# A hybrid convolution and dilated-attention layer on one core: the attention's first unit 32 convolution steps later, and GpSimd's dense-key copies behind a unit's zeros

## The chip, the cores and the metric

The kernel runs on one core of a Trainium2 chip. The metric is the device time of one execution in microseconds (us); less is better. The kernel before took 2181.21 us, the median of three runs (2176.76 to 2185.51). One more execution was profiled. The engines are named as the profile names them: PE is the matmul engine (TensorE) and PEld its weight loads, DVE is VectorE, ACT is ScalarE, POOL is GpSimd, and SP is SyncE, which here only issues DMAs.

## The reference

The input is a sequence of 4096 rows of 1024 float32 values. One combined projection of the normalised rows gives two halves of 512 columns: a gated convolution and an eight-head attention.

```python
h = rmsnorm(x, norm_w); proj = h @ w_in              # (4096, 4096)
u, g_b, g_c, z_conv, q, k, v, z_attn = split(proj, 8)
y_conv = g_b * (conv3(g_c * u) + conv_b) * silu(z_conv)     # width-3, depthwise, centred
q, k = per-head rmsnorm(q), rmsnorm(k)               # 8 heads of 64
for window, dilation in ((128, 1), (512, 4), (2048, 16)):
    # keys of one residue class mod dilation: a band of half-width 64 around each query,
    # logits / 8 + T5 relative bias, softmax -> o_i, log-sum-exp lse_i
y_attn = sum_i softmax(lse)_i * o_i * silu(z_attn)
out = x + concat(y_conv, y_attn) @ w_out
```

## The kernel before

The program has three stages. The first reads x tile by tile, normalises it, and computes q, k, v and the attention's gate, and stores them and the normalised, transposed rows (`hT_d`) in device memory. The second computes the attention and, between its pieces, the convolution half's four projections. The third joins the three dilations and multiplies by `w_out`. Products are done in float16 as a high and a low part, so that a product of two tiles is three matmuls.

The order of all instructions is written out by hand: Python calls emit instructions in program order, and every engine and every DMA queue runs its own in that order. So an instruction that waits holds back all that stand behind it on its engine. This holds for POOL and for SP too, which matters here.

**Units.** The attention is 384 units `u` of 128 queries of a pair of heads (`pr`, four pairs), in groups of eight (`b` = 0 to 7). The first 32 of each pair's 96 units have dilation 16 (`U["d"] == 16`), then come 32 each of the other two. For a unit the program does, spread over several turns of the loop over `u`:

- `q_alone(u)` (L1018): POOL copies each head's queries into `qz`, a tile whose other half is zero. It is done five turns ahead.
- `k_dense(u)` (L1031): for dilation 16 only, POOL copies strided keys into dense tiles `kd`: two copies for the first of two units, one for the second. It is done six turns ahead, while the matmuls that read them (L1044, L1045) are issued two turns ahead.
- `qk(u)` (L1044, L1045): PE makes the logits. `logits(u)` (L1057): DVE adds the bias and takes the minimum of the negated logits, into a tile `L`; for one unit in three (`by_pe(u)`: u % 3 == 1) whose keys are fewer than 256, POOL first zeroes the part of `L` that gets no keys (L1053). Both come two turns ahead.
- `exps(u)` (L1066): ACT's exponentials, one turn ahead. `tr_pe(u)` (L1086): for one unit in three, PE transposes `L`, at the end of the turn before. For the others `p_hi` and `p_lo` (L1098, L1108) make float16 parts in a tile `src`, after POOL has zeroed its dead part (L1097), and `tr(u)` (L1112) transposes it by a DMA on SP's queue.
- `av(u)` (L1123 to L1126): PE multiplies by the values, three turns later (`LAG = 3`).

**Filler.** `fill(n)` runs `n` steps of the generator `conv_gen`, each of three matmuls (L854 to L856) with 128x256 results. 32 steps make one block of 128 channels for 256 rows, and 128 steps one of 16 chunks; the whole is 2048 steps, and 24 more of the output product. A block's tail comes in the steps after it, ending in a multiply on POOL (L821). At a chunk's start `load_h` issues the load of a chunk two ahead (L398, on SP's queue). `start` steps are run before unit 0; the units below `mid` = 184 share 1024 - `start` steps, the rest share 1048, half of each unit's in either half of its turn. Units in which the next pair's queries and keys are loaded get 1.2 times as many.

**The start of the attention.** `first_loads` are 20 DMA transposes of queries and keys into `qk` (L661) on SP's queue, three at the end of the first stage and 17 after the first 17 steps of filler. `load_bias(0, 0)`, at the end of turn 4, loads two pieces of the bias on SP's queue into `wst` (L917), and POOL rearranges them into `bt0` (eight copies, L921, and four small memsets, L923).

```python
for u in range(NU):
    p_hi(u); p_lo(u); exps(u + 1); tr(u) if not by_pe(u)
    fill(pers[u] / 2)
    av(u - LAG); q_order(...); q_alone(u + 5)
    k_dense(u + 6)                    # before: here
    qk(u + 2); logits(u + 2)          # logits holds the memset of L
    fill(pers[u] / 2)
    if by_pe(u + 1): tr_pe(u + 1)
    if u == 4: load_bias(0, 0); load_bias(0, 1)
```

Of the kernel before, what the change touches and what calls it, by code (L numbers as in the profile page):

```python
# [65 lines left out]
def tile_hybrid_block(  # L66
# [593 lines left out]
    def load_stacks(pr, j, a, b):  # L660
        nc.sync.dma_start(qk_t[j][:, a:b], qk_d[a:b, pr, 128 * j:128 * j + 128], transpose=True)  # L661
# [49 lines left out]
    def c_room4():  # L711
        M["res", 1] = pb.tile([128, 1024], F32, name="bt")
        M["ja1"] = pb.tile([128, 512], F32, name="bt0")
# [12 lines left out]
    def sz_load(t):  # L726
        nc.sync.dma_start(M["sz", t % 3], sz_d[t * 128:(t + 1) * 128])
# [160 lines left out]
    def fill(n):  # L888
        state["owed"] += n
        while state["owed"] >= 1.0 and not state["done"]:  # L890
            state["owed"] -= 1.0
            if bg:
                bg.pop(0)()
            if todo:
                todo.pop(0)()
            try:
                next(dense)
            except StopIteration:
                state["done"] = True
# [97 lines left out]
    def q_order(u):  # L997

        U = units[u]
        a = 256 * U["grp"] + 32 * U["b"]  # L1000
        QN[u // 2] = [pb.tile([128, 256], F16, name=f"qn{i}", bufs=3) for i in range(2)]
        for i in range(2):
            nc.gpsimd.tensor_copy(QN[u // 2][i].rearrange("p (n r) -> p n r", r=4),
                                  qk_t[i].rearrange("p (r n) -> p n r", r=4)[:, a:a + 64])
# [8 lines left out]
    def q_alone(u):  # L1013
        U = units[u]
        q_t = QN[u // 2] if U["d"] == 1 else qk_t
        for i in range(2):
            half = slice(64 * i, 64 * i + 64)
            nc.gpsimd.tensor_copy(QZ[u % QZB][i][half], cols(q_t[i], U["qc"], half))  # L1018
# [4 lines left out]
    def k_dense(u):  # L1023
        U = units[u]
        if U["d"] != 16:
            return
        a, r = U["grp"] * (S // 4), U["b"] // 2
        if U["b"] % 2 == 0:
            KD[u // 2] = [pb.tile([128, 256], F16, name=f"kd{r}_{j}") for j in range(3)]
        for j in ((0, 1), (2,))[U["b"] % 2]:  # L1030
            nc.gpsimd.tensor_copy(KD[u // 2][j], qk_t[2 + j].rearrange("p (n r) -> p r n", r=4)[:, r, a // 4:a // 4 + 256])  # L1031

    def qk(u):
        U = units[u]
        if U["b"] == 0:
            OT[U["gi"]] = pb.tile([128, 8, 2, DH + 2], F32, name="ot", bufs=2)
        kn = U["kn"]
        both = bank(3 + u % 2, [128, 2, 256])
        p = [both[:, i] for i in range(2)]
        qc, kc = U["qc"], U["kc"]  # L1040
        q_t = QN[u // 2] if U["d"] == 1 else qk_t
        k_t = KD[u // 2] if U["d"] == 16 else qk_t[2:5]
        for i in range(2):
            nc.tensor.matmul(p[i][:, 0:kn], cols(q_t[i], qc), cols(k_t[i], kc), start=True, stop=False)  # L1044
            nc.tensor.matmul(p[i][:, 0:kn], QZ[u % QZB][i], cols(k_t[2], kc), start=False, stop=True)  # L1045
        ST[u] = p

    def logits(u):
        U = units[u]
        ot, kn, p = OT[U["gi"]], U["kn"], ST[u]  # L1050
        L = pb.tile([128, 2, 256], F32, name="L", bufs=LB)
        if by_pe(u) and kn < 256:
            nc.gpsimd.memset(L[:, :, dead(U)], 0.0)  # L1053
        L = L[:, :, U["c0"]:U["c0"] + kn]
        for i in range(2):
            bias = bt[:, U["g"] - 1, i] if U["g"] else bt0[:, i].rearrange("p a b -> p (a b)")
            nc.vector.tensor_tensor_reduce(  # L1057
                out=L[:, i], in0=p[i][:, 0:kn], in1=bias[:, U["b0"]:U["b0"] + kn],
                scale=alpha, scalar=BIG, op0=OP.add, op1=OP.min, accum_out=ot[:, U["b"], i, DH:DH + 1])
        ST[u] = L  # L1060

    def exps(u):
        U = units[u]
        ot, b, L = OT[U["gi"]], U["b"], ST[u]
        for i in range(2):
            nc.scalar.activation(L[:, i], L[:, i], AF.Exp, scale=-1.0,  # L1066
                                 bias=ot[:, b, i, DH:DH + 1], accum_out=ot[:, b, i, DH + 1:DH + 2])
# [3 lines left out]
    def by_pe(u):  # L1071
        return u % 3 == 1
# [4 lines left out]
    def dead(U):  # L1077
        c0 = 192 if U["c0"] == 0 else 0
        return slice(c0, c0 + 64)
# [8 lines left out]
    def p_hi(u):  # L1088
        U = units[u]
        if by_pe(u):  # L1090
            PT[u] = pb.tile([128, 2, 2, 2, 128], F16, name="pt", bufs=PTB)
            nc.scalar.activation(PT[u][:, 0].rearrange("p a b q -> p (a b) q"), ST[u], AF.Copy, scale=P_SCALE)
            return
        src = src_of(u)
        c = slice(U["c0"], U["c0"] + U["kn"])
        if U["kn"] < 256:
            nc.gpsimd.memset(src.rearrange("p a b c -> p (a b) c")[:, :, dead(U)], 0.0)  # L1097
        nc.scalar.activation(src[:, 0, :, c], ST[u], AF.Copy, scale=P_SCALE)  # L1098

    def p_lo(u):  # L1100
        U = units[u]
        if by_pe(u):
            hi, lo = (PT[u][:, n].rearrange("p a b q -> p (a b) q") for n in range(2))
            nc.vector.scalar_tensor_tensor(lo, ST.pop(u), P_SCALE, hi, op0=OP.mult, op1=OP.subtract)
            return
        c = slice(U["c0"], U["c0"] + U["kn"])
        src = src_of(u)
        nc.vector.scalar_tensor_tensor(src[:, 1, :, c], ST.pop(u), P_SCALE, src[:, 0, :, c], op0=OP.mult, op1=OP.subtract)  # L1108

    def tr(u):  # L1110
        PT[u] = pb.tile([128, 2, 2, 2, 128], F16, name="pt", bufs=PTB)
        nc.sync.dma_start(PT[u].rearrange("p a b c q -> p (a b c) q"), src_of(u).rearrange("p a b c -> p (a b c)"), transpose=True)  # L1112

    def av(u):
        U = units[u]
        pt = PT.pop(u)
        vt = VT[U["gi"]]
        p = bank(6 + u % 2, [128, 2, DH])
        for i in range(2):
            for j in range(2):  # L1120
                v = vt[:, U["vidx"][j], i * 128:i * 128 + 128]
                hi, lo = (pt[:, n, i, j, :] for n in range(2))
                nc.tensor.matmul(p[:, i], hi, v[:, 0:DH], start=j == 0, stop=False)  # L1123
                nc.tensor.matmul(p[:, i], hi, v[:, DH:], start=False, stop=False)  # L1124
                nc.tensor.matmul(p[:, i], lo, v[:, 0:DH], start=False, stop=j == 1)  # L1125
        nc.scalar.activation(OT[U["gi"]][:, U["b"], :, 0:DH], p, AF.Copy)  # L1126
# [14 lines left out]
            nc.scalar.dma_start(dap(o_d0[grp], base, [[R, 128], [128 * R, 8], [1, RW]]), src)  # L1141

    NU = len(units)
    start, mid = 112, 184
    weight = [1 + (0.2 if u % 96 >= 70 and u < 288 else 0) for u in range(NU)]
    pers = [w * steps / sum(ws) for ws, steps in ((weight[:mid], 1024 - start), (weight[mid:], 1024 + 24)) for w in ws]
    fill(17)
# [14 lines left out]
    for u in range(NU):  # L1162
        U = units[u]
        p_hi(u)
        p_lo(u)
        if u + 1 < NU:
            exps(u + 1)
        if not by_pe(u):
            tr(u)
        fill(pers[u] / 2)  # L1170
        if u >= LAG:
            av(u - LAG)
        if u + QZB + 2 < NU and units[u + QZB + 2]["d"] == 1 and units[u + QZB + 2]["b"] % 2 == 0:
            q_order(u + QZB + 2)
        if u + QZB + 1 < NU:
            q_alone(u + QZB + 1)
        if u + 6 < NU:
            k_dense(u + 6)
        if u + 2 < NU:
            qk(u + 2)  # L1180
        if u + 3 == NU:
            c_room2()
            sz_load(0)
        if u + 2 < NU:
            logits(u + 2)
        if u + 3 == NU:
            c_room4()
        if u > 8 and U["b"] == LAG + 1:
            o_store(U["gi"] - 1)
        if U["b"] == LAG and U["gi"] + 1 < len(groups):  # L1190
            VT[U["gi"] + 1] = load_v(*groups[U["gi"] + 1])
        fill(pers[u] / 2)
        if u + 1 < NU and by_pe(u + 1):
            tr_pe(u + 1)
        if state["done"]:
            for _ in range(4):
                if bg:
                    bg.pop(0)()
        pr = U["pr"]
        if u == 4:  # L1200
            load_bias(0, 0)
            load_bias(0, 1)
        for a, b, at, rate in CHUNKS:
            p, n = divmod(u - at, 96)
            for n in range(rate * n, min(5, rate * n + rate) if 0 <= p < 3 else 0):
                load_stacks(p + 1, n, a, b)
        n = u - LAG
        if n > 0 and n % 32 == 0 and n // 32 <= 9:
            load_bias((n - 32) // 96 + 1, order[0][(n // 32 - 1) % 3])
# [107 lines left out]
```

## Time and profile before

| what | value |
|---|---|
| median of three runs | 2181.21 us (2176.76 to 2185.51) |
| the profiled execution's own time | 2186.28 us |
| its span, first to last instruction | 2184.5 us |
| mean granted PE clock | 0.987 of full speed |
| PE busy | 2081.3 us, 95% |
| DVE, ACT, POOL busy | 66%, 49%, 39% |
| first filler step to unit 0's first matmul | 722.0 to 759.2 us |
| first and last PE transposes of a unit (L1086) | 764.5 to 1821.1 us |

In the profile "busy" of PE is the union of modelled matmul times: a matmul is drawn longer than its distance to the next one, so that a gap of PE that is shown is shorter than the time lost. In lines of waits the columns are the engine and line that waited, what ended the wait, and total us, count and longest. In a timeline they are start, duration, engine, line, operation and tiles, with idle time before it in brackets. In a table of stretches each engine's busy us stand with its number of instructions, and the granted clock, the DMA engines' share and GB/s at the end.

### The profile page before, as it was taken

The page shows a single profiled execution, that of the slowest core. Times are in us where ns is not written, and L with a number is a line of the kernel's source. Part 1 is how long each engine was busy: PE and PEld are TensorE (multiplying, and loading weights), DVE is VectorE, ACT ScalarE, POOL GpSimd, SP SyncE. Part 2 cuts the span into 40 slices and gives each one's busy share as a digit, 9 for nine tenths or more (in the row PEclk, how much of TensorE's full clock was granted, in tenths as well). Part 3 has the DMA queues.
Part 4 walks back from the last instruction along what each step waited for, and adds up shares of the span by engine and source line. Part 5 has one row for each costly group of instructions (what it writes and reads, how often), then busy time and mean ns, then how long its engine had stood idle before and what let it go on. Part 6 is the DMA issues. An engine that isn't in the chain of part 4 may idle for free. (4 is left out here: it accounts for less than half of the span.)

```text
span 2184.5 us, 48540 instructions
## 1 busy us (share of the span) xinstructions
PE 2081.3 (95%) x17462; PEld 1533.7 (70%) x17462; DVE 1441.1 (66%) x4032; ACT 1069.4 (49%) x3095; POOL 851.8 (39%) x1635
## 2 busy tenths in 40 slices
PE   7699999999999989998999999999999999999999
PEld 3244444444444778888888888888888887788887
DVE  7755666656665366766677656675667676887776
ACT  6323333433432167666677656666667674222221
POOL 0322232332323265433554346433453454343332
PEclk9899999999999999999999999999999999999999
DMA  5255489975554877799877998769977687787775
GB/s 204 88 153 174 142 176 172 221 177 161 169 169 137 179 138 164 147 164 186 164 160 137 172 194 136 153 120 176 204 141 129 122 171 225 233 256 244 244 244 183
DMA packets 692397, 378.34 MB, mean 173 GB/s; under 512 B 470721, under 2 KB 636732, under 8 KB 688060
## 3 DMA queue, kind: packets, MB, share of 16 engines
q1 hardware_dynamic: 570788, 304.72, 62.0%
q10 hardware_dynamic: 121368, 70.53, 13.7%
q8 instruction: 137, 2.24, 0.4%
q14 instruction: 104, 0.85, 0.1%
HBM read 157.77 MB, written 110.39 MB: 123 GB/s over the span
## 5 line engine op out<-in xcount | busy, mean ns | idle before, releaser
L854 PE MATMUL bank<-hb,w 128*128 128x256 f16 x2048 | 560.9, 274 | 0.3 <-ACT cu L861 0.3
L856 PE MATMUL bank<-hb,w 128*128 128x256 f16 x2048 | 560.8, 274 | 0.0
L855 PE MATMUL bank<-hb,w 128*128 128x256 f16 x2048 | 560.8, 274 | 0.0
L410 PE MATMUL bank<-wa,hb 128*128 128x512 f16 x1024 | 391.4, 382 | 14.9 <-DMA hb<-xs 11.4
L1057 DVE CUSTOM_DVE_ANT_0 L<-bank,bt,alpha 128x256 f32<-128x256 f32 (+1 forms) x768 | 319.0, 453 | 126.3 <-PE bank L1045 74.1
L1066 ACT ACTIVATE L<-L,ot 128x256 f32<-128x256 f32 (+1 forms) x768 | 364.2, 476 | 60.0 <-DVE ot L1057 58.4
L412 PE MATMUL bank<-wa,hb 128*128 128x512 f16 x1024 | 391.2, 382 | 0.8 <-DMA hb<-xs 0.7
L411 PE MATMUL bank<-wa,hb 128*128 128x512 f16 x1024 | 390.9, 382 | 0.3 <-DVE wa L301 0.2
L1018 POOL COPY qz<-qk 64x128 f16<-64x128 f16 x512 | 163.9, 320 | 152.9 <-PE bank L1045 134.6
L1108 DVE SCALAR_TENSOR_TENSOR src<-L,src 128x512 f16<-128x512 f32 (+1 forms) x256 | 171.3, 669 | 71.6 <-ACT src L1098 67.5
L856 PEld LDWEIGHTS <-w 128*128 128x128 f16 x2048 | 201.2, 98 | 24.0
L855 PEld LDWEIGHTS <-w 128*128 128x128 f16 x2048 | 201.2, 98 | 22.8 <-issue 0.5
L854 PEld LDWEIGHTS <-w 128*128 128x128 f16 x2048 | 201.3, 98 | 20.7
L238 POOL TENSOR_TENSOR rs_rq<-rs_mq,mhalf 128x8 f32<-128x8 f32 x64 | 104.9, 1639 | 268.4 <-DVE rs_mq L237 261.4
L410 PEld LDWEIGHTS <-hb 128*128 128x128 f16 x1024 | 101.6, 99 | 136.4 <-DMA hb<-xs 13.8
L1123 PE MATMUL bank<-vt,pt 128*128 128x64 f16 x1536 | 176.6, 194 | 18.9 <-DMA pt<-src 16.3
L412 PEld LDWEIGHTS <-hb 128*128 128x128 f16 x1024 | 100.6, 98 | 125.3 <-issue 4.4
L411 PEld LDWEIGHTS <-hb 128*128 128x128 f16 x1024 | 100.8, 98 | 123.5 <-issue 5.5
L1125 PE MATMUL bank<-vt,pt 128*128 128x64 f16 x1536 | 176.6, 194 | 0.0
L1124 PE MATMUL bank<-vt,pt 128*128 128x64 f16 x1536 | 176.5, 194 | 0.0
L1098 ACT ACTIVATE src<-L 128x512 f16<-128x512 f32 (+1 forms) x256 | 148.4, 580 | 52.4 <-issue 25.2
L441 ACT ACTIVATE h<-wk 128x512 f16<-128x512 f32 x64 | 40.3, 630 | 257.2 <-DVE wk L437 152.3
(211 smaller groups left out, 4440.1 us busy)
## 6 DMA issues: line engine op xcount, KB each, us to landing
o_d<-ot ACTq DMA_DIRECT2D x32, 528.0 KB, 6.1
qk<-o_d SPq DMA_DIRECT2D x63, 264.0 KB, 4.4
hT<-hb SPq DMA_DIRECT2D x16, 1024.0 KB, 4.1
wst<-in_w_in_dram SPq DMA_DIRECT2D x64, 256.0 KB, 3.2
hb<-hT SPq DMA_DIRECT2D x16, 1024.0 KB, 6.4
qk<-in_x_dram SPq DMA_DIRECT2D x32, 512.0 KB, 5.5
qk_d<-h SPq DMA_DIRECT2D x128, 96.0 KB, 2.1
vt<-v_d ACTq DMA_DIRECT2D x48, 256.0 KB, 5.8
```

The source lines that it names most:

```text
L410: nc.tensor.matmul(p, hi[:, kt, :], w[:, 0], start=kt == 0, stop=False)
L411: nc.tensor.matmul(p, hi[:, kt, :], w[:, 1], start=False, stop=False)
L412: nc.tensor.matmul(p, lo[:, kt, :], w[:, 0], start=False, stop=kt == KT - 1)
L854: nc.tensor.matmul(pt, w_h, hi[:, :, kt], start=kt == 0, stop=False)
L855: nc.tensor.matmul(pt, w_h, lo[:, :, kt], start=False, stop=False)
L856: nc.tensor.matmul(pt, w_l, hi[:, :, kt], start=False, stop=kt == KT - 1)
L1057: nc.vector.tensor_tensor_reduce(out=L[:, i], in0=p[i][:, 0:kn], in1=bias[:, U["b0"]:U["b0"] + kn], scale=alpha, scalar=BIG, op0=OP.add, o ...
L1066: nc.scalar.activation(L[:, i], L[:, i], AF.Exp, scale=-1.0, bias=ot[:, b, i, DH:DH + 1], accum_out=ot[:, b, i, DH + 1:DH + 2])
L1108: nc.vector.scalar_tensor_tensor(src[:, 1, :, c], ST.pop(u), P_SCALE, src[:, 0, :, c], op0=OP.mult, op1=OP.subtract)
L1123: nc.tensor.matmul(p[:, i], hi, v[:, 0:DH], start=j == 0, stop=False)
L1124: nc.tensor.matmul(p[:, i], hi, v[:, DH:], start=False, stop=False)
L1125: nc.tensor.matmul(p[:, i], lo, v[:, 0:DH], start=False, stop=j == 1)
```

## The change

Two edits. `start` goes from 112 to 144, so that 32 more steps of the filler run before unit 0, and units 0 to 183 share 880 steps in place of 912 (880/912 = 0.965 of the filler in each). `mid` and all that comes from unit 184 on stay. And `k_dense(u + 6)` is emitted after `logits(u + 2)` in place of before `qk(u + 2)`; on POOL, the only engine of the copies, this puts them behind the memset of `L` in turns that have one. The copies of units 0 to 5, ahead of the loop, stay.

```diff
-    start, mid = 112, 184
+    start, mid = 144, 184
...
         if u + QZB + 1 < NU:
             q_alone(u + QZB + 1)
-        if u + 6 < NU:
-            k_dense(u + 6)
         if u + 2 < NU:
             qk(u + 2)
...
         if u + 2 < NU:
             logits(u + 2)
+        if u + 6 < NU:
+            k_dense(u + 6)
```

How the instructions stand, first on SP's queue, at the first units. `qk` are the queries and keys of `first_loads` (the last two of the 20 are seen), `hb<-hT` is the load of a convolution chunk, `pt<-src` are the transposes of units 0, 2 and 3, and `wst` and `bt` the bias loads of turn 4. Rows with a minus are the order before, with a plus the order after.

```order
 L661 DMA_TRANSPOSE qk_6567<-qk_d 128x1024
 L661 DMA_TRANSPOSE qk_6568<-qk_d 128x1024
-L1112 DMA_TRANSPOSE pt<-src_6574 128x8x128
-L1112 DMA_TRANSPOSE pt<-src_6575 128x8x128
-L1112 DMA_TRANSPOSE pt<-src_6576 128x8x128
-L398 DMA hb_7224<-hT_62 128x4096
+L398 DMA hb_7074<-hT_62 128x4096
+L1112 DMA_TRANSPOSE pt<-src_6574 128x8x128
+L1112 DMA_TRANSPOSE pt<-src_6575 128x8x128
+L1112 DMA_TRANSPOSE pt<-src_6576 128x8x128
 L917 DMA wst<-bv_d 128x256 x2
 L913 DMA bt<-bv_d 128x256 x2
```

The chunk load, which stood directly ahead of the bias loads, now stands ahead of the three transposes, since the 128th filler step comes before unit 0.

Next POOL at turns 4 to 6, before. `bt` and `src` are the bias and the zeroes of unit 5, `qz` the queries of unit 10, `kd_2` the keys of unit 11, `L` the zeroes of unit 7.

```order
L923 MEMSET bt_6573 128x4x16 x2
L1097 MEMSET src_6574 128x4x64
L1018 COPY qz_0_6584<-qk_6559 64x128
L1018 COPY qz_1_6585<-qk_6560 64x128
L1031 COPY kd_2_7275<-qk_6568 128x256
L1053 MEMSET L 128x2x64
L1097 MEMSET src_6575 128x4x64
```

The same place after.

```order
L923 MEMSET bt_6573 128x4x16 x2
L1097 MEMSET src_6574 128x4x64
L1018 COPY qz_0_6584<-qk_6559 64x128
L1018 COPY qz_1_6585<-qk_6560 64x128
L1053 MEMSET L 128x2x64
L1031 COPY kd_2_7395<-qk_6568 128x256
L1097 MEMSET src_6575 128x4x64
```

The memset of `L` goes one copy up; the bias copies, ahead of both, stay where they were.

## The prediction

> **What bounds the kernel now.** I read the page's first section, then a table of stretches by stage, then PE's waits in the units that the change thins, and last the timelines of SP, POOL and PE at the one long wait among them.
>
> ```profile
> span 2184.5 us, 48540 instructions
> PE 2081.3 (95%) x17462; PEld 1533.7 (70%) x17462; DVE 1441.1 (66%) x4032; ACT 1069.4 (49%) x3095; POOL 851.8 (39%) x1635
> ```
>
> PE bounds the whole. Neither edit takes a matmul away, so only PE's idle time (and its clock) can change. The table of stretches says where that is: filler alone, three stretches of some 64 units each, and the output stage.
>
> ```profile
> 723.00:756.00 33.00, 32.66 (x300) 29.13 (x298) 9.75 (x36) 2.84 (x6) 2.73 (x3) 1.00 0.97 204
> 788.00:953.00 165.00, 159.23 (x2001) 142.35 (x1999) 115.40 (x394) 115.27 (x401) 88.27 (x230) 1.00 0.75 146
> 1047.00:1213.00 166.00, 159.30 (x2019) 143.31 (x2016) 117.13 (x400) 117.12 (x407) 89.15 (x238) 1.00 0.79 153
> 1309.00:1489.00 180.00, 171.35 (x2096) 152.58 (x2095) 118.97 (x406) 117.45 (x409) 88.71 (x235) 0.98 0.77 143
> 1869.00:2180.00 311.00, 310.81 (x1365) 257.30 (x1365) 234.27 (x485) 80.52 (x142) 116.02 (x83) 0.99 0.77 240
> ```
>
> First the length, then PE busy. Filler alone leaves PE idle 0.34 of 33 us, the output stage 0.19 of 311. The units leave it idle 5.8, 6.7 and 8.7 us. The next view is PE's waits from unit 0 to about unit 184, where the filler gets thinner.
>
> ```profile
> PE bank L1123 <- DMA pt<-src: 11.1, 10, 2.9
> PE bank L1086 <- ACT L L1066: 8.0, 14, 1.0
> PE bank L1086 <- POOL L L1053: 6.7, 5, 5.3
> PE bank L1045 <- POOL qz L1018: 1.9, 1, 1.9
> PE bank L1123 <- ACT ct L866: 1.6, 1, 1.6
> PE bank L1123 <- ACT ot L1126: 0.5, 1, 0.5
> ```
>
> These are 29.8 us in 32 waits. Two thirds are many short ones, for a transpose by DMA or for the exponentials. One is long: 5.3 us for a memset of POOL. The timelines of SP, POOL and PE show it.
>
> ```profile
> 766.33 5.16 SPq L1112 DMA_TRANSPOSE pt<-src  x3
> 771.58 1.07 SPq L398 DMA_DIRECT2D hb<-hT  x1
> 772.70 0.90 SPq L917 DMA_DIRECT2D wst<-bv_d  x2
> ...
> 776.33 0.77 POOL L1031 COPY kd<-qk 128x256 f16<-128x256 f16 x2
> 779.66 1.44 POOL L921 COPY bt<-wst 128x128 f32<-128x128 f32 x4 [2.55 <-DMA wst<-bv_d]
> ...
> 783.78 0.40 POOL L1031 COPY kd<-qk 128x256 f16<-128x256 f16 x1
> 784.12 0.20 POOL L1053 MEMSET L<- 128x128 f32 x1
> ...
> 778.76 0.27 PE L1086 MATMUL bank<-identf,L 128*128 128x128 f32 x1
> 784.38 0.69 PE L1086 MATMUL bank<-identf,L 128*128 128x128 f32 x2 [5.34 <-POOL L L1053]
> ```
>
> PE comes to unit 7's transpose at 778.8 and stands until 784.4. POOL stood idle 2.55 us for the bias that SP had asked for at 772.7, then worked 4.7 us (779.66 to 784.32) through the bias copies, unit 5's zeroes, unit 10's queries and one dense copy, and only then zeroed unit 7's `L`. SP issued the bias late because the chunk load, 1.1 us of issue, stood ahead of it.
>
> **Part 1: 32 steps before unit 0.** Their price first, from the filler matmuls of one line (one in three) in the same stretches, then the `av` matmuls of one line, four to a unit.
>
> ```profile
> 723.00:756.00 33.00, 27.08 (x100) 9.68 (x99) 1.00 0.97 204
> ...
> 788.00:953.00 165.00, 82.42 (x303) 29.55 (x302) 1.00 0.75 146
> 1047.00:1213.00 166.00, 82.85 (x304) 29.74 (x304) 1.00 0.79 153
> 1309.00:1489.00 180.00, 90.11 (x327) 32.23 (x326) 0.98 0.77 143
> ...
> 1047.00:1213.00 166.00, 28.99 (x256) 23.43 (x254) 1.00 0.79 153
> 1309.00:1489.00 180.00, 29.89 (x258) 24.22 (x259) 0.98 0.77 143
> ```
>
> 100 steps in 33 us are 0.33 us a step, so 32 steps are 10.5 us. That is added ahead of unit 0, where PE has next to no idle time, and taken from 184 units, 0.057 us from each. If those stay bound by PE it cancels. If they are bound by the chain through DVE, ACT and the DMAs, taking filler away only makes PE wait, and up to 10.5 us are lost. The stretches decide: with 304 steps for 64 units PE idles 6.7 us, with 327 for about 64.5 it idles 8.7 us. Denser filler did not cover more waits, so thinner need not uncover more; scaled to 32 steps that comparison would even give 2.7 us back (1.95 x 32/23). The count of waits says a little against: 26 short waits in 184 units (the lines for DMA, exponentials, tanh and `ot`), so one unit in seven is held by a chain, and 26/184 of 10.5 is 1.5 us lost. I take +1.5, nearer to the stretches' row than to the end, and keep -2.7 and +10.5.
>
> The order of the first units' DMAs moves as well. The chunk load goes ahead of the three transposes, into the time that unit 0 now comes later (10.5 us), in which SP has nothing else to do after its stack loads. So the bias is issued 1.1 us earlier relative to unit 4. Its landing is the next question. The issues of that line around unit 4, and then those for the next two pairs:
>
> ```profile
> DMA to landing us min/median/max: 6.9/6.9/6.9
> ...
> DMA to landing us min/median/max: 4.3/4.5/4.6
> ```
>
> The first one shared the engines with a chunk load issued 1.1 us ahead of it and with the end of the stack loads; both are now over by then. At 4.5 us the bias would be there 1.1 + 2.4 = 3.5 us earlier, but POOL was idle only 2.55 us, so its chain moves up 2.55 us. That is this term's cap; if the landing stays at 6.9 us it is 1.1 us. The Trainium skill, DMA: Bandwidth & Descriptors, section Queues, rings and completion order, says that each DMA engine takes the descriptors of one issuing queue in ring order; by that the chunk's must go first and 2.55 us is right. Its section Issuing engines are not separate DMA queues says that queues of different issuers interleave on the same engines; ACT still issues the values' loads at that place, and if they are what slowed the bias, 1.1 us is right. No run here shows yet which; the later rows of 4.3 to 4.6 us lie at turns with the same value loads.
>
> **Part 2: the copies behind the zeroes.** At unit 7's memset one copy (783.78 to 784.12, 0.34 us) is taken from ahead of it. With part 1 the wait goes from 5.34 to 5.34 - 2.55 - 0.34 = 2.45 us: 2.9 us gained. For a bound below, 1.1 + 0.34 = 1.4; nothing at all if the value loads hold the bias even longer; above, the whole 5.34. Elsewhere the four other waits for that memset sum to 6.7 - 5.34 = 1.4 us; only where a dense copy stands directly ahead (dilation 16) can the edit help, and then by one or two copies. I take 0.4 us, ends 0 and 1.4. The copies themselves are delayed by one memset of 0.20 us and are read four turns later, some 10 us at 166 us for 64 units: that costs nothing. No other POOL instruction lies between the old place and the new, and in two turns of three there is no memset, so the order on POOL stays.
>
> **The clock.** Behind the long wait the granted clock fell. Stretches right behind three waits, and the two shorter waits themselves:
>
> ```profile
> 784.00:787.30 3.30, 2.92 (x24) 2.48 (x25) 0.69 (x1) 1.53 (x6) 3.04 (x11) 0.51 1.00 125
> 1004.00:1007.00 3.00, 3.00 (x39) 2.76 (x38) 2.59 (x10) 1.47 (x5) 0.00 (x0) 1.00 0.84 168
> 1725.90:1729.30 3.40, 3.40 (x28) 2.68 (x26) 2.24 (x10) 3.06 (x11) 3.17 (x8) 0.50 0.58 122
> ...
> 1003.11 0.20 PE L1123 MATMUL bank<-vt,pt 128*128 128x64 f16 x1 [2.47 <-DMA pt<-src]
> 1724.60 0.44 PE L1086 MATMUL bank<-identf,L 128*128 128x128 f32 x2 [1.88 <-ACT L L1066]
> ```
>
> Half clock for 3.4 us is 1.7 us of PE's work. After a wait of 1.88 us it came, after one of 2.47 us it did not, so a wait of 2.45 us keeps it with even odds: 0.85 us gained, ends 0 and 1.7. The Trainium skill, TensorE: Matmul & The Clock Gate, section Why this matters for your kernels, puts the idle gap that throttles at about 3 us; the row of 1.88 us disagrees. By the page the full 1.7 us would be gained and the sum would be 0.85 us lower.
>
> **The sum.** -2.9 (the wait) - 0.85 (the clock) - 0.4 (other memsets) + 1.5 (thinner filler) = -2.65 us. Against the profiled execution's 2186.28 that is 2183.6; that execution was 5.1 us above the median of the runs, and 2181.2 - 2.65 = 2178.5. The wait of 1.9 us for `qz` at the first unit stays: the first POOL work still comes at the same place of a block (112 and 144 are both 16 steps into one).
>
> **Rivals.**
>
> - *Units held by the chain.* All the thinner filler turns into waits, and the longest of these pass the point at which the clock falls. Place: `av` and PE's transposes in units 8 to 183. Price: 10.5 us, and half clock behind three more waits, 5.1, less the gains at the start, 3.75: 11.9 us slower, 2193. It decides once most units, not one in seven, wait. The 26 short waits speak for it, the idle time of the denser stretch against.
> - *Nothing moves at unit 7.* The bias lands as slowly as before behind the value loads. The gain there is 1.4 us without the clock, and -1.4 - 0.4 + 1.5 leaves 2181. For it: DMA share 0.97 before unit 0 and 0.75 in the units, so transfers collide everywhere. Against: 4.3 to 4.6 us later.
> - *Faster by more.* The whole wait goes, with its clock (7.0), all other memsets' waits (1.4), and the thinner stretch idles less as the comparison has it (2.7): 11.1 us faster, 2170. It needs POOL to be free before 777, which the row of its copy at 776.33 speaks against.
>
> **How the numbers follow.** The forecast has 0.56, nothing at unit 7 0.24, faster by more 0.11, held by the chain 0.07, and 0.02 is left for something unseen. 0.5% is 10.9 us, about what a measurement of this kernel can tell from no change. The forecast and the second rival lie within it. So faster 0.11, same 0.82, slower 0.07. The likeliest case's own range, from its terms' nearer ends, is 2175 to 2182. For 8 in 10 the ends of the terms count: low 2181.2 - 7.0 - 1.4 - 2.7 = 2170, high 2181.2 + 10.5 - 1.4 = 2190; the faster rival's price lies at the low end.
>
> **What would show it.** In the changed profile unit 0's first matmul comes some 10.5 us later, near 769.7; the chunk load stands ahead of the first transposes by DMA on SP; the bias lands within 5 us; PE's wait at L1086 for L1053 near 790 is 2 to 3 us, and the stretch behind it is at full clock or not. Between unit 8 and unit 184 the short waits sum to within a few us of what they were. The forecast is wrong if those waits grow by more than about 5 us, if falls of the clock become more frequent there, or if POOL's own queue, not the bias, holds unit 7.

## The result, and the profile after

The changed kernel took 2199.67 us, the median of four runs (2197.74 to 2201.43), against 2180.89 for the kernel before (2176.76 to 2185.51, four runs): a ratio of 1.0085, 95% interval 1.0069 to 1.0101. It is 18.8 us slower. The forecast was 2178.5, at most 2190.

The profiled execution's page, first section:

```profile
span 2198.8 us, 48579 instructions
PE 2084.9 (95%) x17462; PEld 1533.0 (70%) x17462; DVE 1444.7 (66%) x4032; ACT 1067.5 (49%) x3095; POOL 855.6 (39%) x1635
```

The shares say nothing: every engine is as busy as before. The table of stretches does, from the first unit's product to unit 184's, first of before and then of after; the first two figures behind the stretch are its length and PE busy.

```profile
770.00:1276.00 506.00, 477.97 (x5960) 428.83 (x5959) 338.20 (x1152) 336.11 (x1164) 244.06 (x659) 0.99 0.86 160
...
780.00:1292.00 512.00, 472.06 (x5855) 420.40 (x5852) 336.29 (x1144) 332.80 (x1161) 246.46 (x659) 0.99 0.83 155
```

The stage begins 10 us later, as the edit says, but then takes 6 us more in place of 10.5 us less. PE has 105 matmuls fewer in these records and idles 39.9 us in place of 28.0. PE's waits in the stage after, to be held against those shown for before:

```profile
PE bank L1123 <- DMA pt<-src: 12.3, 13, 1.9
PE bank L1086 <- ACT L L1066: 11.4, 13, 2.0
PE bank L1086 <- POOL L L1053: 6.8, 5, 3.9
PE bank L1123 <- ACT ot L1126: 4.3, 3, 2.1
PE bank L1123 <- ACT L L1066: 2.4, 1, 2.4
PE bank L1086 <- POOL src L1097: 1.6, 1, 1.6
PE bank L1045 <- POOL qz L1018: 0.9, 1, 0.9
PE bank L1044 <- DVE ot L1057: 0.6, 2, 0.4
```

The waits for transposes by DMA are nearly what they were (12.3 us, 11.1 before). The waits for ACT, at L1086 and L1123, grew from 10.1 us (8.0, 1.6 and 0.5) to 18.1. Unit 7's wait is still there. Its timelines on SP, POOL and PE:

```profile
766.68 0.52 SPq L398 DMA_DIRECT2D hb<-hT  x1
775.36 6.54 SPq L1112 DMA_TRANSPOSE pt<-src  x3
781.95 1.15 SPq L917 DMA_DIRECT2D wst<-bv_d  x2
...
787.99 1.46 POOL L921 COPY bt<-wst 128x128 f32<-128x128 f32 x4 [1.39 <-DMA wst<-bv_d]
...
792.12 0.20 POOL L1053 MEMSET L<- 128x128 f32 x1
792.39 0.41 POOL L1031 COPY kd<-qk 128x256 f16<-128x256 f16 x1
...
788.20 0.27 PE L1086 MATMUL bank<-identf,L 128*128 128x128 f32 x1
792.38 0.90 PE L1086 MATMUL bank<-identf,L 128*128 128x128 f32 x3 [3.91 <-POOL L L1053]
```

The order on SP and POOL is the one announced, and the wait is 3.91 us, not 5.34 and not the 2.45 forecast.

Where ACT is late is seen on its own timeline in the turn of unit 27, where it issues the eight value loads of the first group of dilation 1 in one go. First before, then after; `ACTq` rows are DMA issues, which do not count as busy.

```profile
836.81 0.33 ACTq L949 DMA_DIRECT2D vt<-v_d  x1
...
840.39 0.43 ACTq L949 DMA_DIRECT2D vt<-v_d  x1
841.91 0.32 ACTq L952 DMA_DIRECT2D vt<-v_d  x1
842.28 0.60 ACT L1092 ACTIVATE pt<-bank 128x512 f16<-128x512 f32 x1 [5.20 <-DMA vt<-v_d]
...
847.31 0.33 ACTq L949 DMA_DIRECT2D vt<-v_d  x1
...
850.21 0.54 ACTq L949 DMA_DIRECT2D vt<-v_d  x1
854.08 0.32 ACTq L952 DMA_DIRECT2D vt<-v_d  x1
...
854.92 0.60 ACT L1092 ACTIVATE pt<-bank 128x512 f16<-128x512 f32 x1 [7.34 <-DMA vt<-v_d]
...
856.61 0.19 PE L1123 MATMUL bank<-vt,pt 128*128 128x64 f16 x1 [2.11 <-ACT ot L1126]
```

ACT computes nothing for 5.2 us before and 7.3 after; the last of the eight issues followed the end of the seventh by 1.1 us in the kernel before and by 3.3 in the changed one. Behind it PE waits for ACT's eviction of a product. At the four such turns below unit 184 ACT stood 5.2, 4.5, 4.1 and 4.1 us before, and 7.3, 5.2, 5.5 and 4.1 after, so the holds themselves grew by 4 us; why is not shown. They made the theory that the experiments below tested last.

### The profile page after: what moved, and what is told of

Read it like the earlier page. It is cut to its first block, busy times and chain, and to the rows that moved or that the text cites. A ratio compares the mean times of both kernels' runs of the same rounds, so it can differ in the third digit from the quotient of the medians.

```text
span 2198.8 us, 48579 instructions
## 1 busy us (share of the span) xinstructions
PE 2084.9 (95%) x17462; PEld 1533.0 (70%) x17462; DVE 1444.7 (66%) x4032; ACT 1067.5 (49%) x3095; POOL 855.6 (39%) x1635
## 5 line engine op out<-in xcount | busy, mean ns | idle before, releaser
L1123 PE MATMUL bank<-vt,pt 128*128 128x64 f16 x1536 | 176.0, 194 | 26.8 <-DMA pt<-src 19.2
L1123 PEld LDWEIGHTS <-pt 128*128 128x128 f16 x1536 | 142.2, 98 | 35.7 <-DMA pt<-src 29.7
```

## The experiments

Ratios are to the kernel before on the same chip, with 95% intervals.

**One edit at a time, and the filler without the shift.** Theory A: with thinner filler the units' waits are no longer covered. Theory B: the moved transfers collide. Theory C: the dense copies hold POOL up.

```diff
 e1   start 112 -> 144; k_dense stays ahead of qk
 e2   start 112; k_dense behind logits
 e3   start 144, both edits; steps of units 0-183 / the rest: 912 / 1016 (changed kernel: 880 / 1048)
 e4   start 112; k_dense stays; steps 880 / 1080
```

> The change without its second edit: start is 144, the dense-key copies stay ahead of qk. Theory A (the filler taken from units 0 to 183 no longer covers their waits) and theory B (the convolution's transfers, one block of 32 steps earlier against the units, collide with the units' own) both expect the changed kernel's time, 2197 to 2202 us. Theory C (the dense-key copies behind the memset hold POOL up for something) expects the time of before, 2177 to 2184.

> Only the second edit: start is 112, the dense-key copies come behind logits. Theories A and B expect the time of before, 2178 to 2184 us, since neither filler nor transfers move. Theory C expects 2195 or more.

> The changed kernel, but units 0 to 183 keep 912 steps between them as before, and the 32 steps come out of units 184 to 383 (1016 in place of 1048). So the convolution stands exactly one block further at each of the first 184 units, and the phase of blocks against units is that of before. Theory A expects most of the loss gone: 2181 to 2188 us (the later, denser units may lose a little). Theory B expects the loss to stay, 2196 to 2203. Theory C the same as B.

> The kernel before with thinner filler alone: start stays 112 and the copies stay, units 0 to 183 get 880 steps, units 184 to 383 get 1080. Theory A expects 2193 to 2202 us, nearly the whole loss, less what the denser later units hide. Theories B and C expect the time of before, 2178 to 2185.

Measured: e1 1.0074 (1.0053 to 1.0095), e2 0.999 (0.9977 to 1.0004), e3 1.001 (0.9995 to 1.0024), e4 1.0078 (1.0063 to 1.0093). The copies do nothing that can be measured, so C is out. Thinner filler alone, with nothing moved ahead of unit 0, makes nearly the whole loss, and with the old amount the shift costs nothing that can be measured in sum: A. One reserve on e3: in its own profile the time from unit 0's eviction of products to unit 184's is 513 us, where the same measure gives 505 before and 512 after, and the later, thinner units give it back, so its total is kinder to A than its parts. The same stretch in e4:

```profile
771.90:1291.20 519.30, 476.13 (x5853) 422.10 (x5851) 337.02 (x1143) 332.56 (x1162) 244.06 (x657) 0.98 0.84 154
```

It should have become 10.5 us shorter than before and became 13.9 longer. PE idles 43.2 us in place of 28.0, and the granted clock fell to half six times, for 23.9 us in all, where it fell twice before, for 6.8 us; at half rate 17.1 us more cost up to 8.5.

**The amount.** Theory D: the loss goes with the number of steps taken away. Theory E: it hangs on how blocks of steps fall against units.

```diff
 e5   start  96 (928 steps in units 0-183)
 e6   start 128 (896)
 e7   start 160 (864)
 e8   start 144 (880), weight of units 70-95 and 166-183: 1.2 -> 1.1
```

All four keep the copies behind the zeroes, as in the changed kernel.

> start 96: units 0 to 183 share 928 steps, more than before (912); the copies behind logits. Theory D (the loss grows with the amount of filler taken away) expects it at or a little below the time of before, ratio 0.994 to 1.001. Theory E (the loss hangs on how blocks of 32 steps fall against the units, which every rate sets anew: 6.65 units per block here, 6.77 before, 7.01 in the changed kernel) can't say the sign: anything from 0.995 to 1.01.

> start 128: 896 steps, half of the step from before to the changed kernel, 6.89 units per block. Theory D expects half the loss, ratio 1.003 to 1.006. Theory E expects no particular place between; near 1.000 or near 1.008 would speak for it.

> start 160: 864 steps, half as much again taken away as in the changed kernel, 7.14 units per block. Theory D expects 1.010 to 1.014. Theory E expects it to be as likely below the changed kernel's 1.0085 as above, if 7.01 was an unlucky rate.

> The changed kernel (880 steps in units 0 to 183), but units 70 to 95 and 166 to 183 get 1.1 and not 1.2 times as many as the others, so the others get 4.67 a unit and not 4.56 (4.73 before; 6.85 units per block). Theory D expects the others' loss to shrink to about a third and the heavy units to lose: 1.004 to 1.009 in sum. Theory E expects a value apart from 1.0085.

Measured: 928 steps 1.0025 (1.0006 to 1.0044), 896 steps 1.0018 (0.9998 to 1.0038), 864 steps 1.0055 (1.0038 to 1.0073), and 880 in the other division 1.0076 (1.0048 to 1.0104). Neither theory stands alone: D missed 928, 896 and 864, and E's only firm expectation, a value apart from 1.0085 for e8, did not come. The thin kernels lose (896 steps by no more than the noise), but 864 loses no more than 880, and denser filler, 928, gains nothing. One reading, which these four runs do not show, is that single events are being met, some of which a rate hits and some it misses.

**The events.** Theory F: they are ACT's holds in the eight value loads, eight times in the program (in the turns of units 27, 51, 123, 147 and on). Theory G: the holds only lie there by chance.

```diff
 e9, e10   (on the changed kernel, on the kernel before)
-   nc.scalar.dma_start(vt[rows, ...], v_rows(...))     # eight in a row
+   LATER.append((vt[rows, ...], v_rows(...)))
...
             VT[U["gi"] + 1] = load_v(*groups[U["gi"] + 1])
+        late_loads(2)                                   # two a turn, on ACT's queue as before
 e11       (before) each of the four larger loads cut in two: twelve issues, the same bytes
 e12       (changed kernel) weight + 0.8 in units 28-30, 52-54, 124-126, 148-150; still 880 steps
```

> The changed kernel, but the eight value loads that ACT issues in one go for the first and last group of dilation 1 (units 27, 51, 123, 147, ...) are issued two a turn over four turns. Theory F (what the thinner filler no longer covers is ACT standing for 4 to 7 us in these issues) expects a good part of the loss back: ratio to before 1.000 to 1.005. Theory G (the holds of ACT only happen to lie there; the loss is spread over all waits) expects 1.007 to 1.010.

> The kernel before with the same spread of the eight value loads. Theory F expects a small gain, 0.995 to 0.999, since the filler of before covers most of the holds. Theory G expects 0.999 to 1.002.

> The kernel before with the same value loads cut into twelve issues in place of eight at those eight turns of the program, about 4 x 0.5 us more of ACT's queue each, same bytes. Theory F expects ACT's longer holds to go past what the filler covers: 1.003 to 1.007. Theory G expects 1.000 to 1.002.

> The changed kernel with the same 880 steps in units 0 to 183, but the units right behind the four turns with eight value loads (28 to 30, 52 to 54, 124 to 126, 148 to 150) get 1.8 times as many as the others, which get 5% less than in the changed kernel. Theory F expects 1.003 to 1.007. Theory G, with the others thinner still, expects 1.009 or more.

Measured: e9 0.9965 (0.9948 to 0.9982), e10 0.9925 (0.9897 to 0.9952), e11 1.0081 (1.0049 to 1.0114), e12 1.003 (1.0013 to 1.0046). All four went F's way, and three of them further than F's range; e12 lies at its edge. Spreading the issues takes back more than the whole loss; four more issues at each place give the kernel before the loss of the thin filler; and the same 880 steps cost 0.3% when more of them stand behind the holds. The table of stretches over the four times eight units that begin at units 24, 48, 120 and 144, from eviction to eviction, shows the place. The sum lines, in the order before, after, e9, e10, e11:

```profile
sum 85.68, PE 81.98 PEld 73.26 DVE 60.14 ACT 58.11 POOL 44.54; mean PE 20.49 PEld 18.32 DVE 15.03 ACT 14.53 POOL 11.14
...
sum 94.39, PE 82.22 PEld 71.83 DVE 56.66 ACT 58.64 POOL 44.88; mean PE 20.56 PEld 17.96 DVE 14.17 ACT 14.66 POOL 11.22
...
sum 82.55, PE 78.22 PEld 69.53 DVE 57.75 ACT 58.20 POOL 44.69; mean PE 19.56 PEld 17.38 DVE 14.44 ACT 14.55 POOL 11.17
...
sum 81.83, PE 81.08 PEld 73.14 DVE 60.50 ACT 58.57 POOL 45.92; mean PE 20.27 PEld 18.29 DVE 15.13 ACT 14.64 POOL 11.48
...
sum 92.17, PE 82.59 PEld 73.13 DVE 60.25 ACT 58.22 POOL 44.44; mean PE 20.65 PEld 18.28 DVE 15.06 ACT 14.55 POOL 11.11
```

These 32 units took 85.7 us before and 94.4 after, 8.7 us of the change; 92.2 with twelve issues; 81.8 and 82.6 with the issues spread, where thin or dense filler hardly differs. PE's idle time in them is the length less PE busy: 3.7, 12.2, 4.3, 0.8 and 9.6 us.

Two things limit what this says of the change. First, the changed kernel's longer holds are not needed for a loss: e8 loses 0.76% with holds of 5.0, 4.5, 3.8 and 4.7 us there, as long in sum as before. Second, much of what spreading gains lies where the change thins nothing. In their profiles e9 takes 9.1 us less than the changed kernel from unit 0's eviction to unit 184's, and 12.7 us less from there to the last unit's. So the gain is no measure of the loss; the distance between thin and dense filler is.

**All value loads spread.** With the eight loads spread, thin and dense filler still differ by 0.4% (e9 against e10), where they differed by 0.85%. So on these medians about half of the change's loss goes with the rows of eight issues. The next two spread all groups' loads, one a turn (the eights two a turn); e13 is the changed kernel, e14 the one before.

> The changed kernel with every group's value loads spread: one a turn (two a turn where there are eight). If the 7 us left are ACT's smaller holds, it comes to within 0.1% of the next kernel, some 0.989 to 0.994 of before. If they are other waits, it stays about 0.3% above the next kernel, 0.994 to 0.997 of before.

> The kernel before with every group's value loads spread in the same way. If ACT's smaller holds still cost something with the dense filler, 0.988 to 0.992; if not, the 0.9925 of the kernel with the eight loads alone spread.

Measured: e13 0.9901 (0.988 to 0.9922), e14 0.9851 (0.9828 to 0.9873; 2154.07 us against 2187.28). The smaller holds did cost time in both. But the two stay 0.5% apart: what is left between thin and dense filler, the other half of the loss, is not ACT's standing in a row of issues. PE's waits of e14 in units 0 to about 184, complete:

```profile
PE bank L1129 <- DMA pt<-src: 17.9, 15, 2.6
PE bank L1092 <- POOL L L1059: 3.7, 1, 3.7
PE bank L1092 <- ACT L L1072: 0.4, 1, 0.4
```

(L1129 and L1092 are `av` and PE's transposes there.) The waits for ACT, 10.1 us in the kernel before, are 0.4. What is left is for transposes by DMA, 17.9 us in place of 11.1, and for unit 7's zeroes. The last two runs ask whether the rest of the loss is a straight line in the steps.

```diff
 e15   e14 with start 128 (896 steps)
 e16   e14 with start  96 (928 steps)
```

> The kernel before with all value loads spread (e14) and start 128: 16 of its 32 steps moved ahead. If every step taken from the units is lost at 0.33 us, it stands 5.3 us above e14: 0.9851 + 0.0024 = 0.9875 of before, 0.986 to 0.989. If it is one unlucky rate, 0.984 to 0.986 or 0.990 and more.

> The same with start 96: 16 steps more in the units. On the straight line it is 5.3 us below e14, 0.9827 of before, less what unit 0 loses because the loads of queries and keys still fill SP's queue until 766 us and unit 0's transpose stands behind them (up to 5 us): 0.982 to 0.986.

Measured: e15 0.985 (0.9816 to 0.9883), e16 0.9885 (0.9862 to 0.9908). A straight line is unlikely: 112 and 128 measure the same and 96 and 144 each lose 0.3 to 0.5%, but e15's interval still holds the line's 0.9875, and e16's only just clears its range. (At 144 the copies also stand behind the zeroes, which e2 showed to weigh nothing.) Why 144 loses that, with ACT's holds gone, stays open. The kernel with all value loads spread and start 112 beats both kernels of this case by 1.5 and, over the runs' ratios, 2.3%.

## Why the prediction was wrong, point by point

**The step that failed is the price of the thinner filler, +1.5 us.** Measured alone (e4) it is 0.78%, some 17 us, so the 10.5 us kept as its upper end was no bound either: in e4's profile the time of the 32 steps comes back as waiting, and more waiting and more half clock come on top. The mechanism was that of the rival "units held by the chain", which had 0.07 and 2193 us: the thinner filler turns into waits and falls of the clock. Its condition, that most units wait, was not needed. What ACT's eight issues in a row explain of the loss is about half (0.85% between thin and dense filler with them, 0.4% with them spread); which waits make the other half stays open. The two signs that the prediction named for this case came: leaving out unit 7 and the first unit, PE's waits in the stage grew from 22.6 to 35.5 us, and past unit 7 the clock fell twice in the stage in place of once.

Two things in the working were unsound. The comparison of stretches (304 steps with 6.7 us idle, 327 with 8.7) took two places with different events for two doses of one cause. And the count of 26 short waits gave the share of units held now, not of those that would be with less cover: a wait that the filler of before just hides shows in no line of PE's waits. ACT's four holds in these units were in the trace of before, the first as 5.20 us, and on no view that the prediction used: DMA issues are not busy time, and ACT read as 49%. The prediction reads SP's queue at length and ACT's not at all in these turns. e10 shows what spreading them is worth even before the change: 0.75%.

**The start.** Unit 0's first matmul came at 770.3, forecast 769.7, and the chunk load stood ahead of the first transposes: right. The wait at unit 7 fell by 1.4 us, not by 2.9. The bias landed 5.6 us after its issue, between the 6.9 and the 4.5 used; the view of its line, after:

```profile
DMA to landing us min/median/max: 5.6/5.6/5.6
```

And the 1.1 us of earlier issue did not come: SP's three transposes now took 6.54 us in place of 5.16, ending at 781.9, so the bias was issued 9.25 us later than before, and PE came to unit 7's transpose 9.4 us later. The POOL chain ahead of the memset did shrink by one copy. The wait for `qz` at the first unit did not stay at 1.9 us; it was 0.9.

**The clock.** Even odds were given to no fall behind unit 7. It fell, and for twice as long as before. Stretches of after, behind waits of 3.91 us, 1.77 us, 2.41 us and 2.05 us, with the three shorter waits:

```profile
791.50:798.30 6.80, 5.92 (x38) 4.72 (x39) 2.32 (x7) 3.14 (x11) 5.67 (x18) 0.50 0.42 80
1122.70:1126.00 3.30, 3.30 (x27) 2.50 (x26) 0.76 (x2) 2.32 (x7) 2.84 (x8) 0.50 0.43 83
1149.00:1152.40 3.40, 2.84 (x33) 2.41 (x34) 3.20 (x12) 2.85 (x11) 1.85 (x5) 1.00 0.60 113
1191.00:1194.30 3.30, 3.30 (x26) 2.55 (x25) 1.98 (x6) 2.50 (x9) 1.89 (x4) 0.50 0.39 73
...
1121.34 0.33 PE L1086 MATMUL bank<-identf,L 128*128 128x128 f32 x1 [1.77 <-ACT L L1066]
1147.33 0.20 PE L1123 MATMUL bank<-vt,pt 128*128 128x64 f16 x1 [2.41 <-ACT L L1066]
1189.29 0.93 PE L1086 MATMUL bank<-identf,L 128*128 128x128 f32 x4 [2.05 <-ACT L L1066]
```

At half rate the 5.9 us in which PE worked there cost 3.0, where 2.9 us had cost 1.5 before. So the two terms of the start, -3.75 in the sum, were about -1.4 + 1.5 = +0.1. That is 4 us of the 21 by which the forecast missed; most of the rest is the filler, some 17 us (e4) in place of 1.5.

**The copies behind the zeroes.** -0.34 at unit 7 and -0.4 elsewhere were claimed; alone the edit measures 0.999 (0.9977 to 1.0004), which agrees and can't be told from nothing.

**The two other rivals** did not come about. "Nothing moves at unit 7" had the gain there right, 1.4 us without the clock, but its price for the filler was the forecast's, and its 2181 us was wrong with it.

## What to carry to other kernels

Filler can be worth much more at a few places than on average (e12: the same 880 steps cost 0.3% and not 0.85% with more of them there): before thinning it, look on every queue, the ones of "idle" engines too, for the longest stretches in which an engine issues DMAs or stands behind one. Holds of 4 to 7 us on an engine that reads as half idle cost time here, and spreading its issues over the turns of a loop gained 1.5% where moving filler had lost 0.85%. A comparison of two stretches of one profile is not a dose-response: the dose changes there together with the place.

## What was not expected of the hardware

In the row of after that is shown above a value load takes ACT 0.3 to 0.5 us to issue, but the last of the eight came 3.3 us after the one ahead of it had ended, with no wait that the trace shows; what held it there is open. The Trainium skill, DMA: Bandwidth & Descriptors, section Issuing engines are not separate DMA queues, calls the issuing sequencer's time "usually small relative to the DMA itself"; here taking that time apart, on an engine others wait for, was worth 0.75% in eight places (e10) and 1.5% in all (e14). The clock fell to half behind waits of 1.77 us (and one of 0.74 us right after it) and 2.05 us, and not behind one of 2.41 us, so the length of a wait alone does not tell. The figure of about 3 us that the prediction cites from the Trainium skill, TensorE: Matmul & The Clock Gate, section Why this matters for your kernels, does not agree with the 2.05.
